# First mixer of a two-layer hybrid decoder: 12 of 16 input blocks multiplied whole, compression in column groups, two convolution steps moved between the steps of the attention

## Chip, cores and metric

One core of a Trainium2 chip runs the whole forward pass for 256 tokens of width 1024. The metric is the device time of one execution in microseconds; the time of a kernel is the median of its runs.

## What is computed

Two layers over a residual stream of 256 tokens. Layer 0's mixer, cut to what matters here:

```python
z = hn @ w_in                                   # hn = rmsnorm(x); 2328 columns
val, gate, q, kc, vc, ks, vs, kw, vw, g = split(z)
a = val * sigmoid(gate)                         # 512 channels
a_out = silu(layernorm(causal_conv31(a)))       # depthwise, 31 taps
k_cmp = gelu(blocks(kc) @ cmp_w1[0]) @ cmp_w2[0]   # 15 blocks of 32 tokens, 2 groups
v_cmp = gelu(blocks(vc) @ cmp_w1[1]) @ cmp_w2[1]
b_out = sigmoid(g) . (attn(q, k_cmp, v_cmp), attn(q, ks, vs), attn(q, kw, vw))
h = x + concat(a_out, b_out) @ w_out
```

Attention has 8 query heads and 2 key heads of 64; with 256 tokens the selected and the window branch both see all earlier tokens. Layer 1 mixes with trailing means instead. After each mixer comes a product-key mixture of 16384 experts (the bulk of the time: every expert's two rows, 512 KB for 128 experts, pass through TensorE), then a gated embedding. Everything is float32.

## The kernel before

Activations lie transposed (channels on partitions, 256 tokens along the row), and weights come in blocks of 128x1024 f32 (512 KB): eight 128x128 pieces that give one 128-column slice of the output. `plan` lists all blocks in order of use; `fetch` loads the next one through the SP queue into a ring of buffers (`RINGS`: 3 in the first mixer, 10 afterwards), and `refill` fetches as long as the ring has room.

There are two ways to multiply a block. **Split** (`u_block`, `mm3`): `prep_h` makes a rounded high half on ScalarE (L184), `prep_l` the low half on VectorE (L197), two blocks ahead, and then frees the ring's buffer; TensorE runs three reduced-precision products for each of the 8 pieces (L225 to L227), the activations being split into hnH and hnL at the start. **Whole** (`u_dense`, L248): eight f32 products straight from the ring's buffer, each of which the trace shows as two instructions; the buffer comes free when they are done. Before the change all 16 blocks of the first mixer's input projection (`win`), the 8 of its output projection (`wout`) and the 8 of the query projection (`wq`) are split; the expert tables are whole.

`mixer_even` first does four convolution groups, each with a value block and a gate block, evacuation, tanh, and the gated input `ap[c]` (L474 to L496). Then the loop over `STEPS` (L748) emits the rest: `C` the compressed keys and values (with shifts of E through POOL's queue), `K` the keys, `Q` the queries, `B` the blocks for the compression, `S` the split of the token weights `wt`, `W` values and gates by token, `M` the compression, `s`, `p`, `w` scores, compressed scores and weighing, `T` the part of the convolution taps that TensorE does (diagonal matrices made on ScalarE, L441; products L442; `PE_TAPS` of them per group), `L` one of three parts of the convolution's norm. The other taps are VectorE instructions (L459), one after another for each group; `taps(n)` emits the next n behind a step (`BEHIND_CONV` 6, `BEHIND_STEP` 3, `BEHIND_HALF` 5). The output projection (L760) takes the attention's four pieces first, then the convolution's.

A compression (`compress`, L565) contracts 32 tokens x 64 channels as 16 products of 30 columns (2 groups x 15 blocks) by 256, accumulated in 30 partitions of one bank; then gelu, two transposes, and the second weight.

The order on the SP and POOL queues is that of the program. On TensorE, VectorE and ScalarE a scheduler orders what is ready by the place in the program; an engine works off its queue in order.

Of the kernel before, what the change touches and what calls it, by code (L numbers as in the profile page):

```python
# [20 lines left out]
T = 256  # L21
# [14 lines left out]
RINGS, ROWBUFS, AHEAD = (3, 10), 7, 8  # L36
# [19 lines left out]
class Trunk:  # L56
# [72 lines left out]
    def plan(self):  # L129
# [22 lines left out]
        self.split_range(0, at["wq", 0] + 7)  # L152
# [90 lines left out]
    def u_dense(self, k, x):  # L243

        w = self.raw_block(k)
        out = self.bank()[:, :ND]
        for kt in range(KT):
            m = self.nc.tensor.matmul(out, w[:, kt * 128:kt * 128 + 128], x[:, kt, :ND],  # L248
                                      start=kt == 0, stop=kt == KT - 1)
        self.last_mm[k] = m  # L250
        self.raw_done(k)
        return out
# [145 lines left out]
    def mixer_even(self, st):  # L398
# [3 lines left out]
        base = self.at["in"]  # L402

# [70 lines left out]
        for c in range(4):  # L474
            pv = self.u_block(base + 2 * c)
# [4 lines left out]
            pg = self.u_block(base + 2 * c + 1)  # L480
# [19 lines left out]
        def in_kc(c):  # L500

            pk = self.u_block(next(nxt))
# [6 lines left out]
            blk.append((mp.tile([128, 16, 2, 15], F32, name=f"blk{c}"), E))  # L509
# [5 lines left out]
        def in_k(c):  # L515
            pk = self.u_block(next(nxt))
# [4 lines left out]
        def blocks(c):  # L521
            bt, E = blk[c]
            for g in range(2):
                v = E[g][:, 1:257].rearrange("p (n r) -> p r n", r=16)
                for hf in range(2):
                    pos = cpos[:, c, hf * 8:hf * 8 + 8, None].to_broadcast([128, 8, 15])
                    nc.vector.tensor_tensor(out=bt[:, hf * 8:hf * 8 + 8, g],
# [4 lines left out]
        def in_q(c):  # L532
            pq = self.u_block(next(nxt))
# [3 lines left out]
        wtH = mp.tile([128, KT, 280], F32R, name="wtH")  # L537
        wtL = mp.tile([128, KT, 280], F32R, name="wtL")
        vt = mp.tile([128, 2, 256], F32, name="vt")
        gt = mp.tile([128, 2, 24], F32, name="gt")  # L540

        def split_wt():
            for hf in range(2):
                s = slice(hf * 4, hf * 4 + 4)
                nc.scalar.activation(wtH[:, s], wt[:, s], AF.Copy)
                nc.vector.tensor_tensor(out=wtL[:, s], in0=wt[:, s], in1=wtH[:, s].bitcast(F32),
                                        op=ALU.subtract)
# [17 lines left out]
        def compress(c):  # L565

            ph = self.bank()
            for lp in range(16):
                nc.tensor.matmul(ph[0:30, :256], blk[c][0][:, lp].rearrange("p g n -> p (g n)"),  # L569
                                 w1[c][:, lp], start=lp == 0, stop=lp == 15)  # L570
            hid = mp.tile([30, 256], F32, name="hid", bufs=1)
            nc.scalar.activation(hid, ph[0:30, :256], AF.Gelu_apprx_tanh)
            pt = self.bank()
            for m in range(2):
                nc.tensor.transpose(pt[:, m * 32:m * 32 + 30], hid[:, m * 128:m * 128 + 128],
                                    self.ident[0:30, 0:30])
            hT = mp.tile([128, 2, 32], F32, name="hT", bufs=2)
            nc.scalar.activation(hT[:, :, 0:30],
                                 pt[:, 0:64].rearrange("p (m n) -> p m n", m=2)[:, :, 0:30], AF.Copy)
# [165 lines left out]
        steps = {"T": pe_taps, "C": in_kc, "K": in_k, "Q": in_q, "B": blocks, "S": split_wt,  # L745
                 "W": in_token, "M": compress, "p": compressed, "s": scores, "w": weigh}
        nxt = iter(range(base + 8, base + 16))
        for step in STEPS:  # L748
# [5 lines left out]
            if step[0] in "CKQWMpsw":  # L754
                taps(BEHIND_STEP)
# [697 lines left out]
```

## Time and profile before

| | us |
|---|---|
| median of 3 runs (lowest, highest) | 1530.15 (1526.87, 1534.93) |
| the profiled execution | 1531.44 |
| its span, first to last instruction | 1529.7 |
| mean granted TensorE clock | 0.993 |

The profile gives, for one execution, busy times of the engines, the waits and what ended them, and the chain of work that ended last. PE is TensorE, PEld its weight loads, DVE VectorE, ACT ScalarE, POOL GpSimd, SP SyncE. A matmul's recorded duration overlaps with the next one's, so the time that it costs is read from one start to the next. A few per cent of the records can be missing: of 108 VectorE taps the trace shows 106. The line in a row is that of the instruction, which may stand in a helper.

### The profile page before, as it was taken

Reading aid. Unit: us, or ns where it says so; the run is one execution under the profiler, and the core shown is the slowest. Engines: PE = TensorE matmul, PEld = TensorE weight load, DVE = VectorE, ACT = ScalarE, POOL = GpSimd, SP = SyncE. Lnnn points to the kernel's source line nnn. Section 1 sums busy time; section 2 is a strip of 40 time slices with the busy share of each in tenths; the row PEclk is TensorE's granted clock in tenths of the full one; section 3 lists DMA queues with packets and bytes.
Section 4 is the critical chain, followed back from the end, with each engine's and each line's share of the span. In section 5 each row is a group of like instructions: output and inputs, shape, how many; then the busy total and the mean of one; then the engine's idle time right before and its main releaser. Section 6 shows DMA issues by size and latency. Waiting matters only on the chain.

```text
span 1529.7 us, 30252 instructions
## 1 busy us (share of the span) xinstructions
PE 1499.5 (98%) x11882; PEld 1457.0 (95%) x11882; DVE 1142.0 (75%) x2752; ACT 684.7 (45%) x864; POOL 446.1 (29%) x406
## 2 busy tenths in 40 slices
PE   8999999999999999999998999999999999999997
PEld 8858999999999999999998999999999999999997
DVE  6997699988876888544448699987886788644446
ACT  6468321358863876000036321248872877000025
POOL 0000014343444333444300004343444333343400
PEclk9999999999999999999999999999999999999998
DMA  6603679999999999999985279999999999999980
GB/s 239 231 1 113 233 238 409 408 408 408 408 396 396 402 381 378 405 409 408 409 347 166 89 231 400 408 409 408 409 388 393 409 380 367 408 408 409 409 315 28
DMA packets 141245, 514.83 MB, mean 337 GB/s; under 512 B 15984, under 2 KB 16240, under 8 KB 140592
## 3 DMA queue, kind: packets, MB, share of 16 engines
q1 hardware_dynamic: 84384, 308.42, 52.6%
q0 software_dynamic: 55568, 202.66, 33.7%
q8 instruction: 94, 1.54, 0.4%
q10 hardware_dynamic: 1152, 1.82, 0.4%
q14 instruction: 47, 0.39, 0.1%
HBM read 511.53 MB, written 1.05 MB: 335 GB/s over the span
## 4 chain that ended last, share of the span: by engine, by line
PE 76%; DMA 12%; DVE 10%; ACT 1%; issue 1%; DVEq 0%; SPq 0%; ACTq 0%
PE bank_a L1015 28%; PE bank_a L248 26%; DMA wx<-in_v 9%; PE bank_g L1246 5%; PE bank_a L225 3%; PE bank_a L226 3%; PE bank_a L227 3%; DMA wx<-in_u 3%; DVE row L1341 2%; PE bank_a L569 1%; DVE rt_tmp L1033 1%; PE bank_a L640 1%; DVE yc L459 1%; PE bank_r L306 1%; DVE wL L197 1%
## 5 line engine op out<-in xcount | busy, mean ns | idle before, releaser
L1015 PE MATMUL bank_a<-z,wx 128*128 128x160 f32 x4096 | 574.6, 301 | 3.9 <-DMA wx<-in_v 1.0
L248 PE MATMUL bank_a<-hn,wx 128*128 128x160 f32 x4096 | 569.8, 300 | 2.1 <-DVE rt_gs L1204 1.2
L1015 PEld LDWEIGHTS bank_a<-z,wx 128*128 128x128 f32 x4096 | 559.3, 190 | 11.1 <-DMA wx<-in_v 11.0
L248 PEld LDWEIGHTS bank_a<-hn,wx 128*128 128x128 f32 x4096 | 558.7, 190 | 4.9 <-issue 1.8
L1235 ACT ACTIVATE o<-sq 128x512 fp8e4<-128x512 f16 x160 | 398.6, 2599 | 46.7 <-DVE sq L1227 46.5
L1314 POOL DMA_INDIRECT row<-in_ur,sp_idx x192 | 228.2, 1188 | 475.4 <-PE bank_a L248 193.7
L1351 DVE SCALAR_TENSOR_TENSOR sp_acc<-row,sp_w,sp_acc 128x1024 f32<-128x1024 f32 x188 | 241.7, 1286 | 153.1 <-DMA row<-in_v,sp_idx 152.4
L1314 POOL DMA_INDIRECT row<-in_v,sp_idx x192 | 210.0, 1094 | 333.8 <-PE bank_a L1015 220.3
L1341 DVE SCALAR_TENSOR_TENSOR row<-row,sp_x 128x1024 f32<-128x1024 f32 x192 | 231.1, 1217 | 31.5 <-DMA row<-in_ur,sp_idx 31.5
L184 ACT ACTIVATE wH<-wx 128x1024 fp32r<-128x1024 f32 (+1 forms) x63 | 65.4, 1042 | 389.0 <-DMA wx<-in_proj 338.1
L1008 ACT ACTIVATE z<-bank_a 128x160 f32<-128x160 f32 x256 | 95.8, 379 | 285.9 <-PE bank_a L248 285.2
L1251 DVE SCALAR_TENSOR_TENSOR z<-bank_g,z 128x512 f32<-128x512 f32 x80 | 93.1, 1163 | 66.2 <-PE bank_g L1246 66.2
L197 DVE TENSOR_TENSOR wL<-wx,wH 128x1024 fp32r<-128x1024 f32 (+1 forms) x63 | 75.8, 1204 | 50.9 <-ACT wH L184 50.4
L225 PE MATMUL bank_a<-hnH,wH 128*128 128x256 f32 x320 | 93.5, 295 | 6.0 <-ACT wH L184 5.6
L227 PE MATMUL bank_a<-hnH,wL 128*128 128x256 f32 x320 | 93.0, 292 | 0.3 <-DVE wL L197 0.3
L226 PE MATMUL bank_a<-hnL,wH 128*128 128x256 f32 x320 | 92.8, 291 | 0.0
L1246 PE MATMUL bank_g<-sq,o 128*128 128x64 f16 x1280 | 89.5, 237 | 0.0
L1246 PEld LDWEIGHTS <-o 128*128 128x128 fp8e4 x1280 | 82.6, 113 | 3.0
L1231 DVE TENSOR_TENSOR sq<-o,gHL 128x512 f16<-128x512 f16 x160 | 68.0, 425 | 11.1
L225 PEld LDWEIGHTS bank_a<-hnH,wH 128*128 128x128 f32 x320 | 63.2, 199 | 7.0 <-ACT wH L184 5.8
L1227 DVE TENSOR_TENSOR sq<-iota,i2T 128x512 f16<-128x512 f16 x160 | 67.2, 420 | 0.0
L227 PEld LDWEIGHTS bank_a<-hnH,wL 128*128 128x128 f32 x320 | 63.6, 199 | 0.7 <-DVE wL L197 0.6
(313 smaller groups left out, 1208.6 us busy)
## 6 DMA issues: line engine op xcount, KB each, us to landing
wx<-in_u SPq DMA_DIRECT2D x256, 512.0 KB, 13.1
wx<-in_v SPq DMA_DIRECT2D x256, 512.0 KB, 11.6
wx<-in_wq SPq DMA_DIRECT2D x16, 512.0 KB, 3.7
wx<-in_gatew SPq DMA_DIRECT2D x16, 512.0 KB, 6.5
wx<-in_win SPq DMA_DIRECT2D x15, 512.0 KB, 6.1
w<-in_cw SPq DMA_DIRECT2D x2, 2048.0 KB, 9.9
wx<-in_wout SPq DMA_DIRECT2D x8, 512.0 KB, 3.8
row<-in_ur,sp_idx POOLq DMA_INDIRECT x192, 9.6
```

What stands on the lines that cost most here:

```text
L225: mm(out, wH, xH, start=start, stop=False, **kw)
L226: mm(out, wH, xL, start=False, stop=False, **kw)
L227: mm(out, wL, xH, start=False, stop=stop, **kw)
L248: m = self.nc.tensor.matmul(out, w[:, kt * 128:kt * 128 + 128], x[:, kt, :ND], start=kt == 0, stop=kt == KT - 1)
L1008: self.nc.scalar.activation(z[i // HB][:, i % HB], ps, AF.Gelu_apprx_tanh)
L1015: m = self.nc.tensor.matmul(acc[kt // 2][:, (kt % 2) * ND:(kt % 2) * ND + ND], w[:, kt * 128:kt * 128 + 128], x, start=b == 0 and kt % 2 == 0,
L1235: nc.scalar.activation(o8.rearrange("p t e -> p e t"), o2, AF.Copy, saturate=False)
L1246: nc.tensor.matmul(ps[k][:, c:c + HB], o8[:, t], og[:, p, :, t], start=p == 0, stop=p == 1)
L1251: nc.vector.scalar_tensor_tensor(v, ps.pop(k).rearrange("p (t b) -> p t b", b=HB), 1.0 / GSCALE, v, op0=ALU.mult, op1=ALU.mult)
L1314: ins = k.nc.gpsimd.indirect_dma_start(out=G, out_offset=None, in_=table, in_offset=bass.IndirectOffsetOnAxis(ap=self.idx[:, c:c + 1], axi ...
L1341: nc.vector.scalar_tensor_tensor(G, G, 1.0, self.x[u], op0=ALU.mult, op1=ALU.mult, accum_out=self.dot[:, col])
L1351: nc.vector.scalar_tensor_tensor(self.acc[u], G, self.w[:, col], self.acc[u], op0=ALU.mult, op1=ALU.add)
```

## The change

Four blocks stay split (`SPLIT = 4`, the first two convolution groups). The other twelve go through `u_whole`, which reads a new copy `hx` of the scaled activations (eight ScalarE copies). The token groups use `wt` whole, so step `S` is gone. The ring has four buffers instead of three. The convolution groups become steps `V0` to `V3` in `STEPS`; `V2` now stands behind `K1` and `V3` behind `M1`; the loads of `w1` move from the convolution groups to `C0` and `C1`. The splits of the output projection start after `V3`. `PE_TAPS` changes from 6 and 8 to 4 and 12. In the compression the 16 products are spread over four groups of 32 partitions; a product with `self.sel[1]`, a 128x32 matrix of four stacked identities, sums the groups and transposes in one step, and gelu follows it.

```diff
-RINGS, ROWBUFS, AHEAD = (3, 10), 7, 8
+RINGS, ROWBUFS, AHEAD = (4, 10), 7, 8
+SPLIT = 4
...
-STEPS = ("T1 Q1 C0 C1 K0 K1 B1 Q0 Q2 T3 B0 S W1 Q3 s0 M0 s1 W0 s2 p0 M1 w0 L w1 s3 p1 w2 L w3 L"
-         .split())
-PE_TAPS = (0, 6, 0, 8)
+STEPS = ("V0 V1 T1 C0 C1 K0 K1 V2 Q0 Q1 B1 B0 s0 W0 M0 s2 Q2 Q3 W1 s1 M1 V3 T3 p0 p1 s3 w0 w1 L w2 L"
+         " w3 L".split())
+PE_TAPS = (0, 4, 0, 12)
...
-        self.split_range(0, at["wq", 0] + 7)
+        self.split_range(0, SPLIT - 1)
...
-    def u_dense(self, k, x):
+    def u_whole(self, k, x, n):
...
+        hx = mp.tile([128, KT, T], F32, name="hx")
...
-        for c in range(4):
-            pv = self.u_block(base + 2 * c)
+        def block(k):
+            return self.u_block(k) if k < SPLIT else self.u_whole(k, hx, T)
+
+        def in_conv(c):
+            pv = block(next(nxt))
...
+            pg = block(next(nxt))
             if c == 0:
                 self.stats_close(st, then=AF.Tanh)
+                for kt in range(KT):
+                    nc.scalar.activation(hx[:, kt], self.h[:, kt], AF.Copy,
+                                         scale=self.vecs[:, V_MIX[0], kt:kt + 1])
...
             if c == 1:
                 nc.sync.dma_start(wt, a["wtok"])
-            elif c > 1:
-                nc.sync.dma_start(w1[c - 2], a["cw1"][c - 2])
-            taps(BEHIND_CONV)
...
         def in_kc(c):
-            pk = self.u_block(next(nxt))
+            pk = self.u_whole(next(nxt), hx, T)
...
-            blk.append((mp.tile([128, 16, 2, 15], F32, name=f"blk{c}"), E))
+            bt = mp.tile([128, 16, 32], F32, name=f"blk{c}")
+            nc.gpsimd.memset(bt[:, :, 30:32], 0.0)
+            blk.append((bt, E))
+            nc.sync.dma_start(w1[c], a["cw1"][c])
...
             for kt in range(KT):
-                self.mm3(pv, self.hnH[:, kt, s], self.hnL[:, kt, s], wtH[:, kt], wtL[:, kt],
-                         kt == 0, kt == KT - 1)
+                nc.tensor.matmul(pv, hx[:, kt, s], wt[:, kt], start=kt == 0, stop=kt == KT - 1)
...
-            ph = self.bank()
+            ph = self.bank()[:, :256]
             for lp in range(16):
-                nc.tensor.matmul(ph[0:30, :256], blk[c][0][:, lp].rearrange("p g n -> p (g n)"),
-                                 w1[c][:, lp], start=lp == 0, stop=lp == 15)
-            hid = mp.tile([30, 256], F32, name="hid", bufs=1)
-            nc.scalar.activation(hid, ph[0:30, :256], AF.Gelu_apprx_tanh)
-            pt = self.bank()
+                q = lp % 4 * 32
+                nc.tensor.matmul(ph[q:q + 32], blk[c][0][:, lp], w1[c][:, lp], start=lp < 4,
+                                 stop=lp >= 12, skip_group_check=True)
+            hid = mp.tile([128, 256], F32, name="hid", bufs=1)
+            nc.scalar.activation(hid, ph, AF.Copy)
+            pt = self.bank()[:, :64]
             for m in range(2):
-                nc.tensor.transpose(pt[:, m * 32:m * 32 + 30], hid[:, m * 128:m * 128 + 128],
-                                    self.ident[0:30, 0:30])
+                nc.tensor.matmul(pt[:, m * 32:m * 32 + 32], hid[:, m * 128:m * 128 + 128],
+                                 self.sel[1], start=True, stop=True)
...
+            nc.scalar.activation(hT.rearrange("p m n -> p (m n)"), pt, AF.Gelu_apprx_tanh)
...
-        nxt = iter(range(base + 8, base + 16))
+        nxt = iter(range(base, base + 16))
...
+            if step == "V3":
+                self.split_range(self.at["wout"], self.at["wq", 0] + 7)
+                self.prep_l(self.at["wout"] + 1)
+            if step[0] in "VCKQWMpsw":
+                taps(BEHIND_CONV if step[0] == "V" else BEHIND_STEP)
```

The steps `K` and `Q` call `u_whole` in the same way, and the blocks of `win` are stored in the order in which `STEPS` names them.

## Rows read from the trace of the kernel before

**Rows 1.** The page, its first part: busy us, share of span, instructions of each engine

```profile
PE 1499.5 (98%) x11882; PEld 1457.0 (95%) x11882; DVE 1142.0 (75%) x2752; ACT 684.7 (45%) x864; POOL 446.1 (29%) x406
```

**Rows 2.** Windows by stage, whole kernel; columns: stretch, length, busy us per engine, clock, DMA

```profile
0.00:28.00 28.00, 22.44 (x134) 21.96 (x135) 15.21 (x44) 17.03 (x33) 3.46 (x13) 0.88 0.59 197
28.00:73.00 45.00, 44.37 (x336) 42.13 (x335) 44.26 (x89) 20.79 (x33) 2.31 (x4) 1.00 0.72 265
73.00:128.80 55.80, 54.25 (x323) 32.62 (x322) 50.02 (x155) 42.52 (x123) 0.00 (x0) 1.00 0.06 20
128.80:152.00 23.20, 23.18 (x192) 23.17 (x193) 19.31 (x38) 16.50 (x33) 0.80 (x2) 1.00 0.52 160
```

**Rows 3.** Groups by line, 28 to 128.8 us: busy, mean ns, idle before

```profile
L459 DVE SCALAR_TENSOR_TENSOR yc<-ap,cvec,yc 128x256 f32<-128x256 f32 x106 | 47.1, 475 | 0.2
L227 PE MATMUL bank_a<-hnH,wL 128*128 128x256 f32 x97 | 27.7, 286 | 0.3 <-DVE wL L197 0.3
L197 DVE TENSOR_TENSOR wL<-wx,wH 128x1024 fp32r<-128x1024 f32 x13 | 15.8, 1217 | 0.3 <-ACT wH L184 0.3
L184 ACT ACTIVATE wH<-wx 128x1024 fp32r<-128x1024 f32 x13 | 13.7, 1056 | 14.8 <-PE bank_a L226 5.3 <-DMA wx<-in_wout 3.4 <-DMA wx<-in_win 3.1
```

**Rows 4.** Chain that ended last, mixer: start us, us to the next piece, what

```profile
30.18 0.12 PE bank_a L225
39.54 0.86 PE bank_g L442 x4
72.09 0.13 PE bank_a L225
...
75.97 7.04 PE bank_a L569 x32
90.90 0.86 PE bank_a L640 x2
118.53 1.75 PE bank_a L684 x16
```

**Rows 5.** Timeline of PE, column groups and tiles: start us, us, line, operands

```profile
107.03 1.08 PE L692 MATMUL bank_g<-PT,vt 128*64 128x256 f32 x8
108.05 0.61 PE L674 MATMUL bank_a<-ident,Pc 128*15 128x128 f32 x4
...
180.39 0.67 PE L1063 MATMUL bank_g<-sub,qT 64*32 64x128 f32 x32
180.99 1.22 PE L248 MATMUL bank_a<-hn,wx 128*128 128x160 f32 x7
```

**Rows 6.** Timelines of DVE and PE, fourth convolution group: evacuation, gating, then its taps

```profile
41.00 0.42 DVE L472 TENSOR_TENSOR th<-bank_a,rs 128x256 f32<-128x256 f32 x1
43.26 0.42 DVE L488 SCALAR_TENSOR_TENSOR ap<-th,val 128x256 f32<-128x256 f32 x1
...
64.10 1.03 PE L442 MATMUL bank_g<-ap,dg 128*128 128x256 f32 x4
67.06 1.13 PE L442 MATMUL bank_g<-ap,dg 128*128 128x256 f32 x4
```

**Rows 7.** Timelines of DVE and PE: last tap, row broadcast, projection start

```profile
107.50 0.48 DVE L459 SCALAR_TENSOR_TENSOR yc<-ap,cvec,yc 128x256 f32<-128x256 f32 x1
125.37 1.41 DVE L734 TENSOR_TENSOR yc<-yc,bank_r 128x256 f32<-128x256 f32 x4 [1.79 <-PE bank_r L338]
...
128.82 0.62 PE L225 MATMUL bank_a<-hnH,wH 128*128 128x256 f32 x3 [0.49 <-ACT hnH L699]
```

**Rows 8.** Waits, 28 to 128.8 us: who for whom, total us, times, longest

```profile
ACT wH L184 <- DMA wx<-in_win: 3.1, 1, 3.1
ACT hT L578 <- PE bank_a L575: 1.6, 2, 1.2
```

**Rows 9.** DMA issues: count, KB each, median us to landing

```profile
wx<-in_win SPq DMA_DIRECT2D x15, 512.0 KB, 6.1
w<-in_cw SPq DMA_DIRECT2D x2, 2048.0 KB, 9.9
```

More of the change, by code (lines that the diff above doesn't have):

```diff
@@ L241, in u_block @@
         return out
-    def u_dense(self, k, x):
+    def u_whole(self, k, x, n):
         w = self.raw_block(k)
-        out = self.bank()[:, :ND]
+        out = self.bank()[:, :n]
         for kt in range(KT):
-            m = self.nc.tensor.matmul(out, w[:, kt * 128:kt * 128 + 128], x[:, kt, :ND],
+            m = self.nc.tensor.matmul(out, w[:, kt * 128:kt * 128 + 128], x[:, kt, :n],
                                       start=kt == 0, stop=kt == KT - 1)
@@ L515, in in_k @@
         def in_k(c):
-            pk = self.u_block(next(nxt))
+            pk = self.u_whole(next(nxt), hx, T)
             for g in range(2):
@@ L526, in blocks @@
                     pos = cpos[:, c, hf * 8:hf * 8 + 8, None].to_broadcast([128, 8, 15])
-                    nc.vector.tensor_tensor(out=bt[:, hf * 8:hf * 8 + 8, g],
+                    nc.vector.tensor_tensor(out=bt[:, hf * 8:hf * 8 + 8, g * 15:g * 15 + 15],
                                             in0=v[:, 0::2, hf:hf + 15], in1=pos, op=ALU.add)
@@ L532, in in_q @@
         def in_q(c):
-            pq = self.u_block(next(nxt))
+            pq = self.u_whole(next(nxt), hx, T)
             nc.vector.scalar_tensor_tensor(qT[c], pq, 0.125, self.rs, op0=ALU.mult, op1=ALU.mult)
-        wtH = mp.tile([128, KT, 280], F32R, name="wtH")
-        wtL = mp.tile([128, KT, 280], F32R, name="wtL")
         vt = mp.tile([128, 2, 256], F32, name="vt")
         gt = mp.tile([128, 2, 24], F32, name="gt")
[L542 to L547, printed above, removed]
         def in_token(tt):
@@ L744, in mixer_even @@
         ln = conv_norm()
-        steps = {"T": pe_taps, "C": in_kc, "K": in_k, "Q": in_q, "B": blocks, "S": split_wt,
+        steps = {"V": in_conv, "T": pe_taps, "C": in_kc, "K": in_k, "Q": in_q, "B": blocks,
                  "W": in_token, "M": compress, "p": compressed, "s": scores, "w": weigh}
-        nxt = iter(range(base + 8, base + 16))
+        nxt = iter(range(base, base + 16))
         for step in STEPS:
@@ L753, in mixer_even @@
                 steps[step[0]](*map(int, step[1:]))
-            if step[0] in "CKQWMpsw":
-                taps(BEHIND_STEP)
+            if step == "V3":
[3 more added lines that the diff above has]
+                taps(BEHIND_CONV if step[0] == "V" else BEHIND_STEP)
         st = self.stats_open()
@@ L898, in peer_and_ple @@
             step(self.GATE_NS if i > HB else self.DENSE_NS if sparse.ready else self.ROUTE_NS)
-            ps = self.u_dense(base + i, hn)
+            ps = self.u_whole(base + i, hn, ND)
             if pend is not None:
@@ L1394, in layout @@
     qh = q.reshape(D, 2, 4, 64)
-    cols = []
-    for c in range(4):
-        cols += [val[:, 128 * c:128 * c + 128], gate[:, 128 * c:128 * c + 128]]
-    named = {"C0": kc, "C1": vc, "K0": ks, "K1": kw}
-    named.update({f"Q{j}": qh[:, :, j].reshape(D, 128) for j in range(4)})
-    cols += [named[n] for n in STEPS if n in named]
+    named = {"C0": (kc,), "C1": (vc,), "K0": (ks,), "K1": (kw,)}
+    named.update({f"Q{j}": (qh[:, :, j].reshape(D, 128),) for j in range(4)})
+    named.update({f"V{c}": (val[:, 128 * c:128 * c + 128], gate[:, 128 * c:128 * c + 128])
+                  for c in range(4)})
+    cols = [x for n in STEPS if n in named for x in named[n]]
     a["win"] = f(np.stack([_cols(c) for c in cols]))
```

3 lines of the change are left out of this document (removed).

## The prediction

> **What bounds the kernel now.** I read the page first [rows 1]: TensorE is busy for 98% of the span. Busy time of pipelined matmuls overstates the work, so the stage has to be read by start-to-start times. The windows by stage [rows 2] are next: the change touches only the first mixer, that is the stretch up to 128.8 us (where the output projection begins), and, through the buffers, the 23.2 us of projection behind it. From 28 us, where the four blocks that stay split have passed, to 128.8 us the reader sees VectorE busy for 94.3 of 100.8 us (44.3 + 50.0), ScalarE for 63.3, and the DMA engines busy for 72% and then 6%. So two engines could be the bound, TensorE and VectorE.
>
> The groups of that stretch [rows 3] say what fills VectorE: 106 recorded convolution taps, 47.1 us; 13 subtractions for the low half of a weight block, 15.8 us. ScalarE spends 13.7 us on the 13 high halves.
>
> For TensorE I add up start-to-start times from the chain and the timeline [rows 4, 5]: a split matmul 0.12 us, so a split block (24) 2.88 us; a 280-column one 0.13 us, so a token group (24) 3.15 us; a convolution tap in whole f32 (two instructions of 256 columns) 0.43 us; a compression 7.04 us; a score product 0.86 us and its mask 0.11; a 128-column transpose 0.11 us; a two-column-group instruction 0.128 us. The stretch from 28 us then holds 12 blocks (34.6), 14 taps (6.0), 2 token groups (6.3), 2 compressions (14.1, and about 1.0 of short products), 12 score products with masks (11.6), 16 products for the compressed scores (1.7, taken at the transpose's 0.11), the weighing with 64 transposes and 64 paired instructions (7.0 + 8.2) and the convolution norm with 8 long and 20 short ones (1.7 + 2.2): 94.4 us of 100.8. **TensorE is the bound**, dense to 94%; about 6.4 us are waits. VectorE is nearly as full but seldom in its way. Everything behind the mixer starts from its last product, and nothing of it is edited, so I carry a microsecond there as a microsecond of the span.
>
> **The change part by part.** *Twelve whole blocks.* Each loses 24 products at 0.12 us (2.88) and gains 8 f32 products of 256 columns. The chain has that shape: the tap, 0.86 us for four instructions with the next following at once, and the compression, 32 in 7.04 [rows 4]. So 16 x 0.216 = 3.46 us, 0.58 more per block, **+6.9 us on TensorE** for twelve. It takes 12 x 1.22 = 14.6 us from VectorE and 12 x 1.06 = 12.7 us from ScalarE [rows 3], two of the twelve ahead of 28 us, and adds eight scaled copies on ScalarE (hx). I cost those at nothing: a copy of 128x1024 takes 1.06 us [rows 3], so eight quarters of it are some 2 to 4 us, ScalarE is idle for 11 of the first 28 us [rows 2], and hx is first read at about 28 us. Without that cover it is those 2 to 4 us, once.
>
> *Token groups whole.* 24 products at 0.13 become 8 f32 products of 280 columns, 16 x 0.216 x 280/256 = 3.78 us instead of 3.15: **+1.3 us** for both. The splitting of wt (four instructions) goes too; none of it is on the path.
>
> *Taps.* PE_TAPS goes from 14 to 16: **+0.9 us** on TensorE, two taps less on VectorE (about 0.9 us).
>
> *Compression in column groups.* Now 32 instructions of 30 output columns, one behind another, in 7.04 us. After the change four neighbours write four groups of 32 partitions. The trace has no such four; it has neighbours. Two groups of 64 (the weighing): 8 instructions in 1.02 us, 0.128 us instead of 0.22 [rows 5], a factor of 1.7 out of 2. Tiles of 64x32: 32 instructions of 128 columns in 0.60 us [rows 5], 0.019 against 0.109 for a whole one [rows 4], 5.8 out of 8. At 0.72 to 0.85 of a factor of 4 a compression takes 2.1 to 2.4 us. Bounds: 1.76 (a full four) and 4.1 (no better than two groups). I take 2.2, the nearest rows being those with several tiles at work: **-9.6 us** for both, between -10.6 and -5.9. The Trainium skill (TensorEngine Tiling (Array Packing), Theoretical Speedup) gives up to 4x for 32 columns; by that the term would be -10.6 us.
>
> The same rows speak against a full gain: eight paired instructions at 0.216 a pair would be 0.86 us, and 1.02 pass before the next form starts [rows 5], some 0.15 us at a change of form. Four such changes are 0.6 us, inside the value taken. The Trainium skill (same page, Key Properties) states that changing the tiling mode drains the engine; the row agrees in kind, and no row here isolates its price.
>
> The sum of the groups moves from a transpose to a product with sel[1], four short instructions instead of two; gelu moves behind it, the copy of 128x256 before it replaces a gelu of the same width. I take these as zero, with 0.3 us either way per compression.
>
> TensorE's work: +6.9 + 1.3 + 0.9 - 9.6 = **-0.5 us**, between -1.5 and +3.2.
>
> *Waits.* Of the 6.4 us, some go: the subtraction of wtL, a tap mixed between split products, and the weight preparation behind ScalarE. Others stay: the two hand-overs to ScalarE inside a compression (1.6 us of idle ScalarE before hT [rows 8] shows their size). I take **-1 us**, between -4 (only the compression's own hand-overs and the switches stay) and 0.
>
> *Order and queues.* Steps V2 and V3 (two blocks each, then tanh and gating) move behind K1 and M1. Each carries its evacuations (L472 to L488), the SP queue's refills, and V3 carries the start of the output projection's splits (two high, two low halves, 2.1 us of ScalarE, 2.4 us of VectorE), now in the last third instead of in the middle. VectorE has some 16 us less to do in this stage, so it hides them. On SP the two loads of w1 (2 MB each) move ahead, behind the fetches that blocks C0 and C1 release; fetches behind them wait. A load of w1 lands in 9.9 us, a block in 6.1 [rows 9]. The ring holds four blocks, so a block's fetch is issued some three blocks (10.4 us) ahead, and by my count the tightest one (the second block of V2) has 4 us left. Zero, with 1 us as the far bound; before the change one such delay was 3.1 us of ScalarE's time and reached nobody [rows 8]. POOL gets two small memsets behind the shifts of E; its queue then only waits for the routing.
>
> **Sum.** -0.5 - 1 = -1.5 us. The profiled execution took 1531.44 us, its span is 1529.7 us, the rest lies around it and is not edited; the median of the three runs is 1530.15, 1.3 us below. On the median: 1530.15 - 1.5, so about **1528.5 us**.
>
> **The rivals.**
>
> *A. The tail becomes the bound (slower).* The convolution of channel group 3 starts only when V3 is done. Adding the steps from 28 us in the new order (T1 1.7, six blocks 20.7, Q0 Q1 6.9, s0 1.9, W0 3.8, M0 3.2, s2 3.9, Q2 Q3 6.9, W1 3.8, s1 1.9, M1 3.2, V3 6.9) V3 ends at 93 us. From the product's evacuation to the gated input takes 2.7 us [rows 6]: 95.7. T3 now has 12 taps; eight took 3.8 us [rows 6], so 12 take 5.7, or up to 7 where other products stand between: 101 to 103. Nineteen VectorE taps follow at 0.40 alone or 0.59 when another instruction stands between: last tap at 109 to 114, against 108.0 now [rows 7]. Between the last tap and the projection lie 20.8 us now (108.0 to 128.8 [rows 7]); kept whole, the projection would get its last inputs 1 to 6 us later than now. For it: 0.5 us of TensorE's wait at 128.82 is already put down to ScalarE's hnH, and VectorE waits 1.8 us for the row broadcast just before [rows 7], so this chain is late now. Against: in those 20.8 us each step waits for weighing steps put ahead of it, counted by their own instructions alone they add to about 14 (an estimate); and the attention halves of the first three projection blocks (3 x 12 x 0.12 = 4.3 us) can run before the convolution's. It decides from a last tap later than about 112 us. Price +2 to +6, at the middle **1534 us**.
>
> *B. The relief counts (faster).* VectorE loses some 16 of 94 us (ten of the twelve subtractions at 1.22, the two of wt at about 1.3, two taps). If the waits fall to their lower bound and the four groups run in full, -1.5 - 4 = -5.5 us: **1524.5 us**. Against: VectorE's fullness shows in few of TensorE's waits now.
>
> *C. The column groups do less than said.* With pairs only the compression gives -5.9 instead of -9.6: work +3.2, waits -1, **1532.5 us**. With none beside another it gives nothing: +9.1 - 1, **1538 us**. The 64x32 rows [rows 5] speak against both.
>
> *D. A transfer is late* behind w1: +3 to +5 us, **1533 us**, against it the 4 us of reserve.
>
> **How the numbers follow.** Forecast (between -4 and +1 us) 0.48, A 0.22, B 0.14, C 0.10 (0.03 of it with no groups at all), D 0.03, something that I don't see 0.03. A measurement can tell 0.5% (7.65 us) from no change, that is under 1522.5 and over 1537.8. Before's own three runs lie 8 us apart, so a true -5.5 is read as faster now and then, and a true +6 as slower: half of B and a little of the forecast make faster 0.11; the worse half of A, the no-groups case of C and a part of what I don't see make slower 0.13; same 0.76. For 8 in 10 the range reaches from B with some spread, 1521, to the far end of A with it, 1537.
>
> **What would show it.** Right: a whole block at 16 instructions in about 3.46 us where now 24 take 2.88; a compression's 32 products in 1.8 to 2.4 us; VectorE's share between 28 and 110 us down from full to about 80%; the projection starting between 125 and 129 us; nothing changed in the stages behind but the offset. A: TensorE idle before the projection, waiting for hnH of the convolution channels, with the last tap behind 112 us. B: a projection that starts before 124 us. C: 32 compression products in 4 or 7 us. D: a wait of TensorE for a transfer of win or of w1. I am wrong in kind if a stage behind the mixer changes its length, or if the clock granted in the mixer does (1.00 from 28 us on [rows 2]).

## The result, and the profile after

The changed kernel takes 1546.99 us (median of 6 runs, 1545.54 to 1551.39), the kernel before in the same series 1530.8 us (6 runs, 1526.87 to 1534.93). The ratio is 1.0116, with a 95% interval of 1.0097 to 1.0136: slower by some 17 us, outside the range that I gave. The profiled execution took 1548.81 us, its span is 1547.0 us, 17.3 more than before.

The windows by stage, core 0 of the changed kernel (stretch, length, busy us of PE, PEld, DVE, ACT and POOL, granted clock, share of the DMA engines, GB/s). The bounds are the first score (63.4), the end of the first attention steps, the end of V3's products (111.5) and the output projection (140.0 to 171.0). Below the dots stand two short stretches at the lower clock:

```profile
29.00:63.40 34.40, 29.71 (x138) 25.55 (x137) 30.17 (x76) 3.46 (x8) 2.57 (x6) 1.00 0.68 252
63.40:84.80 21.40, 17.93 (x86) 9.87 (x86) 17.99 (x47) 10.60 (x37) 0.00 (x0) 0.76 0.00 1
84.80:111.50 26.70, 25.67 (x146) 19.96 (x146) 14.69 (x50) 10.98 (x35) 0.00 (x0) 1.00 0.36 119
111.50:140.00 28.50, 28.50 (x179) 17.93 (x178) 16.60 (x44) 20.95 (x56) 0.00 (x0) 1.00 0.06 19
140.00:171.00 31.00, 27.91 (x202) 27.01 (x202) 22.43 (x50) 20.65 (x40) 0.80 (x2) 0.89 0.35 120
...
64.50:71.40 6.90, 4.83 (x9) 2.67 (x9) 6.02 (x15) 2.84 (x16) 0.00 (x0) 0.51 0.00 0
78.20:81.60 3.40, 3.40 (x13) 1.63 (x13) 2.50 (x8) 1.64 (x4) 0.00 (x0) 0.50 0.02 5
```

Against [rows 2] three things are new. TensorE is idle for 9.2 of the 111.0 us from 29 to 140 (111.0 less 29.71, 17.93, 25.67 and 28.50), before for 2.2 of 100.8. Its granted clock falls to half twice in this stretch, where it was full before. And the projection, 23.2 us long at full clock before, takes 31.0 at 0.89, although nothing in it is edited.

That gives the account. The projection starts at 140.0 instead of 128.8, 11.2 us later: 1.0 from the first whole block (28.95 instead of 28), 7.0 from idle TensorE, 4.1 from the half clock (half of the 4.83 and of the 3.40 us that it worked at it), which leaves -0.9 for the work itself. The projection adds 7.8. From there to the expert tables it is 29.0 us in both. Of the 19.0 us, 17.3 reach the end.

TensorE's timeline (start us, duration us, engine, line, operands, count, and in brackets the idle time before and what ended it):

```profile
28.95 2.32 PE L251 MATMUL bank_a<-hx,wx 128*128 128x256 f32 x10
...
33.27 18.29 PE L251 MATMUL bank_a<-hx,wx 128*128 128x256 f32 x84
52.87 7.14 PE L251 MATMUL bank_a<-hx,wx 128*128 128x256 f32 x32 [1.31 <-DMA wx<-in_win]
63.39 1.10 PE L642 MATMUL bank_a<-kz,qT 128*128 128x512 f32 x2 [3.37 <-DVE qT L544]
...
66.80 2.07 PE L642 MATMUL bank_a<-kz,qT 128*128 128x512 f32 x2 [2.07 <-DVE qT L544]
...
74.09 1.93 PE L571 MATMUL bank_a<-w,blk 128*32 128x256 f32 x32
76.53 0.63 PE L578 MATMUL bank_a<-sel,hid 128*128 128x32 f32 x4 [0.50 <-ACT hid L574]
78.06 0.55 PE L586 MATMUL bank_a<-hT,w 128*64 128x15 f32 x8 [0.90 <-ACT hT L581]
...
104.52 7.17 PE L251 MATMUL bank_a<-hx,wx 128*128 128x256 f32 x32
...
113.36 1.03 PE L446 MATMUL bank_g<-ap,dg 128*128 128x256 f32 x4
...
121.99 0.60 PE L446 MATMUL bank_g<-ap,dg 128*128 128x256 f32 x2
...
146.44 0.63 PE L228 MATMUL bank_a<-hnH,wH 128*128 128x256 f32 x3 [0.90 <-ACT hnH L742]
...
152.93 0.39 PE L228 MATMUL bank_a<-hnH,wH 128*128 128x256 f32 x1 [1.44 <-ACT wH L187]
...
154.19 0.58 PE L230 MATMUL bank_a<-hnH,wL 128*128 128x256 f32 x1 [0.75 <-DVE wL L200]
```

What was costed is as costed: 84 instructions of whole blocks at 0.216 us from one start to the next (18.29 us less the last one's recorded 0.38, by 83), and 32 products of a compression in 1.93 us instead of the 7.04 of [rows 4]. The first scores are what is late: the last query block ends at 59.8, and the two score products with their masks, 1.9 us of work, last until 69.1, with two waits for qT. VectorE's timeline shows why:

```profile
42.05 0.36 DVE L537 TENSOR_TENSOR blk<-E,cpos 128x120 f32<-128x120 f32 x1 [1.54 <-DMA E<-E]
...
45.34 0.36 DVE L537 TENSOR_TENSOR blk<-E,cpos 128x120 f32<-128x120 f32 x1 [1.88 <-DMA E<-E]
...
53.82 0.42 DVE L476 TENSOR_TENSOR val<-bank_a,rs 128x256 f32<-128x256 f32 x1
...
59.14 3.77 DVE L463 SCALAR_TENSOR_TENSOR yc<-ap,cvec,yc 128x256 f32<-128x256 f32 x9
62.82 0.42 DVE L544 SCALAR_TENSOR_TENSOR qT<-bank_a,rs 128x256 f32<-128x256 f32 x1
63.16 3.26 DVE L463 SCALAR_TENSOR_TENSOR yc<-ap,cvec,yc 128x256 f32<-128x256 f32 x8
66.32 0.43 DVE L544 SCALAR_TENSOR_TENSOR qT<-bank_a,rs 128x256 f32<-128x256 f32 x1
...
111.73 0.42 DVE L476 TENSOR_TENSOR th<-bank_a,rs 128x256 f32<-128x256 f32 x1 [3.03 <-PE bank_a L251]
...
122.62 0.48 DVE L460 SCALAR_TENSOR_TENSOR yc<-ap,cvec,bank_g 128x256 f32<-128x256 f32 x1 [0.87 <-PE bank_g L446]
...
133.02 1.52 DVE L463 SCALAR_TENSOR_TENSOR yc<-ap,cvec,yc 128x256 f32<-128x256 f32 x3
```

It stood 3.4 us for the shifts of E, with everything behind it in its queue: the value block of V2 was evacuated at 53.82, though its product had ended at 48. The taps that fill the time of a product each came late too, nine ahead of the first qT and eight ahead of the second. In the last third the fourth group's rows of [rows 6, 7] are found again, much later: its gate block is evacuated at 111.73 instead of 41.00, its twelve taps on TensorE run from 113.36 to 122.5, where eight had begun at 64.10, and VectorE's 19 taps run from 122.6 to 134.5, where the last one was over at 108.0 before. From there to the first product with the convolution's half at 146.44 it is another 11.9 us.

The projection itself then holds 3.1 us of idle TensorE (31.00 less 27.91). Of these, 0.90 are the wait for the convolution's half. The other two waits, 1.44 and 0.75, are for halves of a weight block: ScalarE makes them behind a square of the projection's first result, for which it had stood 1.51 us:

```profile
151.51 0.42 ACT L285 ACTIVATE sq<-h 128x256 f32<-128x256 f32 x1 [1.51 <-DVE h L767]
```

From about 153 to 160 us the clock is at half.

The DMA issues from 28 to 62 us (count, KB each, median us to landing) belong to VectorE's wait and to TensorE's of 1.31 us; the last line is from the same view of the kernel before, in a fence of its own, and blocks of `win` landed in 7.4 us there:

```profile
wx<-in_win SPq DMA_DIRECT2D x8, 512.0 KB, 9.0
w<-in_cw SPq DMA_DIRECT2D x2, 2048.0 KB
E<-E POOLq DMA_DIRECT2D x4, 64.0 KB, 6.4
```

```profile
E<-E POOLq DMA_DIRECT2D x4, 64.0 KB, 4.3
```

### The profile page after: what moved, and what is told of

Same layout as the page of the kernel before. It is cut to its first block, busy times and chain, and to the rows that moved or that the text cites. A ratio compares the mean times of both kernels' runs of the same rounds, so it can differ in the third digit from the quotient of the medians.

```text
span 1547.0 us, 29993 instructions
## 1 busy us (share of the span) xinstructions
PE 1506.3 (97%) x11778; PEld 1459.3 (94%) x11778; DVE 1129.2 (73%) x2736; ACT 673.0 (44%) x858; POOL 450.7 (29%) x408
## 4 chain that ended last, share of the span: by engine, by line
PE 68%; DVE 16%; DMA 12%; ACT 2%; issue 1%; POOL 0%; SPq 0%; DVEq 0%; ACTq 0%
PE bank_a L1020 28%; PE bank_a L251 22%; DMA wx<-in_v 9%; PE bank_g L1251 5%; DVE row L1346 4%; PE bank_a L228 3%; PE bank_a L230 3%; PE bank_a L229 3%; DVE yc L463 2%; DVE rt_tmp L1038 1%; DMA wx<-in_u 1%; DVE rt_ixd L1042 1%; PE bank_a L642 1%; DMA row<-in_ur,sp_idx 1%; PE bank_g L694 1%
## 5 line engine op out<-in xcount | busy, mean ns | idle before, releaser
L1240 ACT ACTIVATE o<-sq 128x512 fp8e4<-128x512 f16 x160 | 398.7, 2600 | 47.0 <-DVE sq L1232 45.8
L187 ACT ACTIVATE wH<-wx 128x1024 fp32r<-128x1024 f32 (+1 forms) x51 | 52.9, 1038 | 383.1 <-DMA wx<-in_proj 337.7
L200 DVE TENSOR_TENSOR wL<-wx,wH 128x1024 fp32r<-128x1024 f32 (+1 forms) x51 | 61.1, 1203 | 51.5 <-ACT wH L187 50.4
L228 PE MATMUL bank_a<-hnH,wH 128*128 128x256 f32 x224 | 66.4, 304 | 8.0 <-ACT wH L187 7.1
L230 PE MATMUL bank_a<-hnH,wL 128*128 128x256 f32 x224 | 66.7, 301 | 1.5 <-DVE wL L200 1.5
L229 PE MATMUL bank_a<-hnL,wH 128*128 128x256 f32 x224 | 66.5, 300 | 0.0
L228 PEld LDWEIGHTS bank_a<-hnH,wH 128*128 128x128 f32 x224 | 45.6, 207 | 8.8 <-ACT wH L187 7.3
## 6 DMA issues: line engine op xcount, KB each, us to landing
wx<-in_v SPq DMA_DIRECT2D x256, 512.0 KB, 10.6
```

What stands on the lines that cost most here:

```text
L228: mm(out, wH, xH, start=start, stop=False, **kw)
L229: mm(out, wH, xL, start=False, stop=False, **kw)
L230: mm(out, wL, xH, start=False, stop=stop, **kw)
L1240: nc.scalar.activation(o8.rearrange("p t e -> p e t"), o2, AF.Copy, saturate=False)
```

## The experiments

The theory behind the first ones: the **order** made the loss. V3 behind M1 makes the convolution's tail late (rival A, larger than I priced it), and the loads of w1, moved ahead, delay what is fetched beside them (rival D). The rivals: the whole blocks cost more than their work, or the column groups give less than their work. Each time stands with its ratio to the kernel before in the same series. The kernel before lay at 1530.8 us beside the changed kernel, at 1527.56 beside w1_late, v3_early, old_order and cmp_alone, at 1530.06 beside both_moved, old_compress, cmp_filled and covered, and at 1530.37 beside the rest, so gains and losses below are differences of ratios, taken of 1530 us. The last two columns and all rows are of one profiled execution, whose own time stands under "profiled" and is up to 6.4 us off the median.

| | us | ratio (95% interval) | profiled | last tap | projection, length |
|---|---|---|---|---|---|
| before | 1530.8 | | 1531.44 | 108.0 | 128.8, 23.2 |
| changed | 1546.99 | 1.0116 (1.0097 to 1.0136) | 1548.81 | 134.5 | 140.0, 31.0 |
| w1_late | 1540.23 | 1.0086 (1.0069 to 1.0102) | 1541.39 | 127.8 | 133.3, 29.7 |
| v3_early | 1531.42 | 1.0027 (1.0011 to 1.0042) | 1531.82 | 90.5 | 129.8, 23.2 |
| both_moved | 1537.5 | 1.0050 (1.0033 to 1.0066) | 1536.43 | 89.4 | 138.6, 23.2 |
| all_split | 1533.15 | 1.0025 (1.0013 to 1.0037) | 1537.8 | 121.5 | 127.5, 30.9 |
| old_compress | 1559.26 | 1.0194 (1.0177 to 1.0211) | 1552.82 | 142.8 | 148.4, 28.4 |
| old_order | 1531.85 | 1.0029 (1.0016 to 1.0042) | 1533.93 | 91.0 | 131.5, 23.2 |
| whole_alone | 1538.09 | 1.0055 (1.0038 to 1.0072) | 1535.98 | 89.3 | 136.6, 23.2 |
| cmp_alone | 1538.34 | 1.0072 (1.0052 to 1.0091) | 1543.67 | 119.4 | 139.2, 27.0 |
| cmp_filled | 1534.34 | 1.0032 (1.0018 to 1.0046) | 1532.0 | 111.2 | 129.6, 25.5 |
| covered | 1543.01 | 1.0091 (1.0072 to 1.0110) | 1540.18 | 88.4 | 137.2, 25.5 |
| lean_old | 1529.4 | 0.9996 (0.9984 to 1.0007) | 1531.18 | 95.4 | 129.1, 23.2 |
| lean_new | 1528.63 | 0.9985 (0.9976 to 0.9995) | 1528.97 | 96.9 | 126.9, 23.2 |

### v3_early

```diff
-... K0 K1 V2 Q0 Q1 ... s1 M1 V3 T3 p0 ...
+... K0 K1 V2 V3 T3 Q0 Q1 ... s1 M1 p0 ...
```

> The changed kernel with V3 and T3 moved up, right behind V2; all else as it is. Theory 2 (late V3): the output projection took 31.0 us instead of 23.2 because the convolution's last taps end 26 us later than before; with V3 early the last tap ends before 115 us, the output projection takes 23 to 25 us, and the time falls by 6 to 9 us, to 1538 to 1541. Theory 1 (transfers at the start) alone: nothing moves at the first scores, the time stays within 3 us of 1547.

Measured: 1.0027, some 13.6 us less than the changed kernel (0.89% of 1530), from two steps of `STEPS` alone. Its windows (columns as above):

```profile
29.00:72.20 43.20, 39.74 (x183) 34.29 (x182) 42.07 (x103) 8.92 (x20) 2.58 (x6) 1.00 0.60 213
72.20:100.70 28.50, 26.98 (x141) 17.99 (x139) 20.05 (x51) 14.53 (x49) 0.00 (x0) 1.00 0.34 112
100.70:129.80 29.10, 28.42 (x222) 18.44 (x221) 17.78 (x70) 25.61 (x73) 0.00 (x0) 1.00 0.00 1
129.80:153.00 23.20, 23.20 (x193) 23.20 (x194) 19.32 (x38) 16.43 (x33) 0.80 (x2) 1.00 0.48 160
```

The projection is back at 23.2 us and the clock full throughout. Last tap and projection are as the theory of the late V3 expected, but the gain is larger than its 6 to 9 us. It is more than the tail: TensorE no longer waits for qT, nor VectorE for the shifts of E. VectorE's adds on E begin at 45.8 there instead of 42.05, and two more blocks pass on TensorE ahead of the queries, in which VectorE can catch up; that this is why is argued, not shown. TensorE's waits fall to 5.7 us (100.8 less 39.74, 26.98 and 28.42), of which 1.71 for a block of win and 1.75 for V3's gating.

### w1_late

```diff
-            nc.sync.dma_start(w1[c], a["cw1"][c])         # in in_kc: C0, C1
+            if step in {'Q0': 0, 'Q1': 1}:
+                nc.sync.dma_start(w1[n], a["cw1"][n])
```

> The changed kernel with one edit: the two loads of w1 (2 MB each) are issued behind Q0 and Q1 instead of behind C0 and C1. Theory 1 (transfers): in the changed kernel the loads of w1 slow the shifts of E and the fetch of Q0's block; VectorE stands 3.4 us for E in its queue and falls about 6 us behind, so Q0's and Q1's evacuations come late and TensorE idles about 7 us at the first scores, where its clock also falls. Then the wait of VectorE for E is gone, the first scores start near 60 us instead of 63.4, and the time falls by 6 to 11 us, to 1536 to 1541. Theory 2 (late third convolution group alone): the loss is in the tail, the time stays within 3 us of 1547. Theory 3 (the planned order of VectorE's queue alone, taps ahead of the evacuations): the first scores still start 3 us or more behind the end of Q1's product, and the time falls by less than 4 us.

Measured: 1.0086, about 4.6 us less than the changed kernel: between what theories 1 and 3 gave. The first score starts at 58.98 instead of 63.39, as theory 1 said. The wait for a block of win, VectorE's for E and the first of the two for qT are gone. The second stays, as TensorE's timeline shows:

```profile
62.29 1.12 PE L641 MATMUL bank_a<-kz,qT 128*128 128x512 f32 x2 [2.07 <-DVE qT L543]
```

So the loads of w1 did hold up the shifts and a block of win. The tail stays late behind the scores: last tap 127.8, a projection of 29.7 us.

### both_moved

Both edits together.

> The changed kernel with both moves undone: V3 and T3 directly behind V2, and the two loads of w1 issued behind Q0 and Q1. If the order alone made the loss (late V3, early w1) and my sum for TensorE holds (-0.5 of work, -1 of waits): the 1.7 us wait for a block of win that was left with V3 early is gone as well, the projection starts at 127 to 129 us and the time is 1527 to 1530 us. If the sum is wrong, because TensorE's waits did not get less: the projection starts at 130 or later, 1531 to 1534 us.

Measured: 1.0050, slower than V3 early alone; both expectations failed, since w1 is now late. The row of TensorE's timeline with the first compression, then the windows around the stretch at half clock:

```profile
82.93 3.64 PE L569 MATMUL bank_a<-w,blk 128*32 128x256 f32 x32 [4.70 <-DMA w<-in_cw]
```

```profile
29.00:80.80 51.80, 47.11 (x212) 39.36 (x210) 50.70 (x124) 14.78 (x43) 2.57 (x6) 1.00 0.44 154
80.80:94.50 13.70, 10.60 (x52) 5.09 (x53) 9.68 (x24) 5.82 (x13) 0.00 (x0) 0.50 0.58 243
94.50:138.60 44.10, 43.42 (x288) 29.71 (x286) 21.22 (x78) 29.12 (x88) 0.00 (x0) 1.00 0.07 25
```

The first load of w1 was issued only at 72.8, behind three refills of the output projection in SP's queue. The wait is 4.7 us, and in the middle of it the clock goes to half for 13.7 us, which costs half of the 10.6 us worked there. The place of these two loads has two wrong sides, ahead of the blocks and behind the refills.

### all_split

```diff
-            return self.u_block(k) if k < SPLIT else self.u_whole(k, hx, T)
+            return self.u_block(k)                         # C, K and Q in the same way
```

> The changed kernel with all 16 input blocks split as before, the new order and the column groups kept. By my sum TensorE has 6.9 us less to do: 1539 to 1541 us. If in this order VectorE's queue is what TensorE waits for (twelve subtractions of 1.22 us more on it, ahead of the same taps): 1548 us or more, the last tap later than 134, the first score later than 63.

The output projection's splits, too, simply follow those of the input blocks here, instead of starting behind V3.

Measured: 1.0025, below both expectations: in the new order the whole blocks cost 13.9 us, not 6.9, although they relieve VectorE. The first score comes at 55.1 instead of 63.4, no wait for a block of win is left, and only 0.3 us of waiting for qT; VectorE's adds on E stand at 57.68 and later instead of from 42.05, behind its subtractions, and wait for nothing. Rows of TensorE, VectorE and the projection's window:

```profile
55.12 1.02 PE L642 MATMUL bank_a<-kz,qT 128*128 128x512 f32 x2
...
57.68 0.35 DVE L537 TENSOR_TENSOR blk<-E,cpos 128x120 f32<-128x120 f32 x1
...
127.50:158.40 30.90, 27.94 (x202) 26.95 (x202) 22.30 (x50) 20.65 (x40) 0.80 (x2) 0.89 0.35 120
```

So a VectorE with more to do is not what TensorE waits for; these rows speak for what stands in its queue ahead of a late transfer, though the edit also changes when buffers come free. The tail stays late all the same: with 12.5 us less in front of it the projection still takes 30.9 us in the profiled execution, which was the longest of the ten, 4.7 us over the median.

### old_compress

The compression of before, in the changed kernel.

> The changed kernel with the compression of before (32 products of 30 columns one behind another) in the new order. V3 still stands behind M1, so all that a compression takes longer delays V3, its convolution and the projection: by the order theory +9.6 us of the two compressions, 1555 to 1558 us, last tap 141 to 146. If the clock behind the column groups costs as much as they save: 1545 to 1550 us, with no half clock between 70 and 85 us.

Measured: 1.0194, 12 us above the changed kernel and somewhat above both ranges, last tap 142.8. By the ratios the column groups give there about what they save (10.2 us, twice 7.04 less 1.93), and the clock doesn't take it back. The profiled execution, the shortest of the four, shows less: its projection starts 8.4 us later than in the changed kernel, and its own time is 4.0 us longer.

### old_order and whole_alone

```diff
-STEPS = ("V0 V1 T1 C0 C1 K0 K1 V2 Q0 ...   PE_TAPS = (0, 4, 0, 12)
+STEPS = "V0 V1 V2 V3 T1 Q1 C0 C1 K0 K1 B1 Q0 Q2 T3 B0 W1 Q3 s0 M0 s1 W0 ..."   PE_TAPS = (0, 6, 0, 8)
```

Both have the order of before, with w1 loaded behind V2 and V3 and the splits of wout behind Q3; whole_alone has the old compression besides.

> The changed kernel (twelve whole blocks, tokens whole, compression in column groups, ring of four) in the old order: all four convolution groups first, the old steps, 6 and 8 taps on TensorE, the loads of w1 behind V2 and V3, the output projection's splits begun behind the last block. If the order is what costs (theories 1 and 2 together), TensorE's sum holds again: 1524 to 1531. If whole blocks themselves cost it (twelve at 3.46 us and a buffer that stays taken until the products are done), it stays at 1540 or above.

> The order and the compression of before, the taps on TensorE of before (14), with twelve whole blocks and whole token groups: what the whole blocks do alone. By my sum +6.9 and +1.3 of work on TensorE, less some waits: 1536 to 1539 us. If VectorE was in TensorE's way in the kernel before (the relief of 16 us counts): 1531 to 1534 us, with the last tap at 90 to 95 instead of 108. Beside the same order with the compression in column groups as well (1531.9 us) it also says what the column groups give there: 9.6 us by my sum, which would be 1541 us here, or next to nothing if the clock takes it back.

Measured: whole_alone 1.0055 (1.0038 to 1.0072), 8.4 us, against +8.2 by my sum (6.9 and 1.3). VectorE's last tap came 18.7 us earlier and that gave nothing: rival B falls. old_order 1.0029, just above the range that the order theory gave: the old order, with its taps and its place of the loads of w1, takes away 13 of the changed kernel's 18 us. The column groups give 4.0 us here, not 9.6, with a clock of 0.91 from 83 to 103 us behind the waits of the first compression.

### cmp_alone and cmp_filled

cmp_alone is the kernel before with the new compression and nothing else. cmp_filled adds products that nobody reads:

```diff
             nc.scalar.activation(hid, ph, AF.Copy)
+            fill = self.bank()[:, :256]
+            for q in range(4):                             # three more behind the product with sel
+                nc.tensor.matmul(fill, self.ident, w1[c][:, q], start=True, stop=True)
```

> The kernel before with one part of the change: the compression in four column groups. If TensorE bounds the mixer before the change, a compression's 32 products take 1.8 to 2.4 us instead of 7.0 and the time falls by 6 to 10 us, to 1521 to 1525. If VectorE bounds it (it is full from 35 to 110 us), TensorE only waits more and the time falls by less than 3 us.

> The kernel before with the compression in column groups alone, and with TensorE kept at work in the compression's two hand-overs to ScalarE: four full products of 128x256 f32 (0.43 us each) behind the 32 products, three more behind the product with sel, into a bank that nobody reads. 3 us of work more in each compression, 6 us together, of which the hand-overs (2.5 us of idle TensorE in each) hide most. If the clock is what made the compression alone slow (granted half for four stretches of 3 to 10 us behind such gaps): the clock stays at full from 23 us to the projection, which starts at 127 to 132 us instead of 139, and the time is 1528 to 1533 us although TensorE has more to do. If VectorE is what made it slow: 1538 to 1543 us, the projection at 139 or later. If both: the clock full and the projection between 133 and 138.

Measured: the compression alone makes the kernel slower, 1.0072, which neither expectation had. With 6 us of useless work added it is at 1.0032: the intervals do not meet. The two kernels are 6 us apart by the ratios; the rows below exaggerate that, because the profiled execution of cmp_alone was the longest of its four and that of cmp_filled a short one of its ten (1543.67 and 1532.0). Windows of cmp_alone, then of cmp_filled:

```profile
73.00:105.00 32.00, 26.95 (x171) 16.46 (x170) 29.34 (x86) 22.62 (x71) 0.00 (x0) 0.81 0.05 16
105.00:139.20 34.20, 30.75 (x150) 17.38 (x149) 17.39 (x63) 18.50 (x46) 0.00 (x0) 0.78 0.05 16
```

```profile
73.00:105.00 32.00, 31.76 (x225) 21.30 (x224) 31.67 (x95) 22.86 (x72) 0.00 (x0) 1.00 0.02 6
105.00:129.60 24.60, 21.41 (x121) 13.84 (x121) 13.90 (x50) 16.92 (x43) 0.00 (x0) 0.86 0.07 23
```

And TensorE's waits around the first and the second compression in cmp_alone:

```profile
78.52 0.63 PE L580 MATMUL bank_a<-sel,hid 128*128 128x32 f32 x4 [1.58 <-ACT hid L576]
80.05 0.62 PE L588 MATMUL bank_a<-hT,w 128*64 128x15 f32 x8 [0.90 <-ACT hT L583]
...
100.70 1.03 PE L678 MATMUL bank_a<-ident,Pc 128*15 128x128 f32 x4 [2.57 <-DVE Pc L626]
```

At the end of its second compression cmp_alone was 7 us ahead of the kernel before (97.5 against 104.5); the rest up to the projection took 41.7 us instead of 24.3. In the old order VectorE is full (29.34 of 32.0), and the faster TensorE waits: 1.58 and 0.90 us for ScalarE inside the first compression, 2.57 for VectorE behind the second. The clock falls to half behind these waits (0.50 from 100 to 106 us), and much of the weighing runs at half. The filling keeps the clock full up to 105 us. About 5 us stay over the kernel before, with 3.2 us of waits for the convolution's norm behind VectorE's last tap (111.2) and a fall of the clock behind them; that this part is VectorE's is argued from these rows. So neither expectation held whole: the projection starts at 129.6, as for the clock alone, but the clock isn't full up to it.

### covered, lean_old and lean_new

```diff
+... K1 V2 V3 Q0 T3 Q1 B1 B0 s0 M0 W0 X0 s2 Y0 Q2 Q3 M1 W1 X1 s1 Y1 p0 ...   # covered: compress cut into M, X, Y; w1 behind Q0, Q1
+PE_TAPS = (0, 4, 0, 4)                                                       # lean_old: old_order
+... K1 V2 V3 Q0 T3 Q1 B1 B0 s0 W0 M0 ...   PE_TAPS = (0, 4, 0, 4)           # lean_new: w1 behind V2, V3
```

> As both moves undone, and besides: T3 one block later (behind Q0, so that TensorE does not wait for V3's gating, 1.8 us), and the compression cut into three steps with other steps between them (M0 W0 X0 s2 Y0 and M1 W1 X1 s1 Y1), so that other products stand in its hand-overs to ScalarE (1.6 to 2.4 us of idle TensorE in each). If the waits of TensorE are what is left: another 3 to 5 us less than with both moves undone, 1523 to 1527 us, the projection at 123 to 126 us. If the end is set by the weighing's own chain (scores, ScalarE, transposes) or by the convolution norm: no less than with both moves undone, 1527 to 1531 us.

Measured: 1.0091. The first compression, now ahead of W0, waited 6.1 us for w1, and the stretch from the second compression to the projection took 35.7 us with TensorE dense; both expectations failed, and whether covered hand-overs help was not settled.

> The order of before with whole blocks and column groups, and 8 instead of 14 taps on TensorE (PE_TAPS 0, 4, 0, 4): VectorE's last tap was at 91 there, some 20 us before it is needed, so TensorE gives it six taps back. If TensorE bounds that order: 6 x 0.43 = 2.6 us less, and up to 1.8 us of its wait for the fourth group's gating, 1527 to 1530 us, last tap at 93 to 97. If VectorE's queue still bounds the stretch up to the scores: no gain, 1531 to 1534 us.

> The changed kernel with V3 directly behind V2, T3 behind Q0, eight taps less on TensorE (PE_TAPS 0, 4, 0, 4) and the loads of w1 behind V2 and V3, between the place that made a block late (behind C0 and C1) and the one that made the compression late (behind Q0 and Q1). If the three waits found (1.7 us for a block of win, 1.8 us for the gating, 4.7 us for w1 with the half clock behind it) are what is left over my sum: full clock from 23 us on, the projection at 123 to 127 us, 1524 to 1528 us. If w1 is late at this place too: TensorE idle before the first compression, half clock behind it, 1532 to 1538 us.

Measured: lean_old 0.9996, no difference from before and 5 us less than old_order, as expected if TensorE bounds that order; its clock still fell around the first compression (0.83 from 80 to 100 us). lean_new 0.9985 (0.9976 to 0.9995), 2 us faster than the kernel before and about 20 faster than the changed one, the projection at 126.9 as expected and the time 0.6 us over its range:

```profile
29.00:69.40 40.40, 39.09 (x183) 33.82 (x183) 39.56 (x100) 4.97 (x12) 2.57 (x6) 1.00 0.62 226
69.40:98.00 28.60, 27.07 (x145) 18.07 (x147) 27.79 (x68) 15.73 (x50) 0.00 (x0) 1.00 0.34 114
98.00:126.90 28.90, 28.24 (x220) 18.29 (x220) 17.57 (x69) 25.43 (x73) 0.00 (x0) 1.00 0.01 1
126.90:150.10 23.20, 23.18 (x192) 23.18 (x193) 19.32 (x38) 16.49 (x33) 0.80 (x2) 1.00 0.50 160
```

TensorE waits for 3.5 of 97.9 us, the clock stays full, and the taps that TensorE no longer does end on VectorE at 96.9, well before they are needed.

## Why the prediction was wrong, by its own steps

**The work was right.** Whole blocks 3.46 us each, as said; token groups 3.77 (said 3.78); a compression 1.93, between the bounds of 1.76 and 4.1 and nearer to the full four than the 2.2 that I took; the work of TensorE together -0.9 us by the account above (said -0.5), and whole_alone at +8.4 for a term of +8.2. VectorE's share from 29 to 111.5 us fell to 76% (said 80% up to 110). The Trainium skill (TensorEngine Tiling (Array Packing), Theoretical Speedup) gives up to 4x for 32 columns; the trace shows 7.04 against 1.93 us, 3.6x.

**"Order and queues" failed.** I costed it at zero because VectorE has 16 us less to do. Two steps of it broke. First, the loads of w1: I looked at the blocks of win behind them (4 us left for the second block of V2, 1 us as the far bound; the trace shows a wait of 1.31, for Q0's block), and passed over POOL's queue, of which I noted two memsets. What was held up there was the shifts of E, and VectorE waited for them, with the evacuations of K0, K1, V2 and the queries queued behind it. That is rival D, by a way that I had not seen: w1_late, which moves only these two loads, gains 4.6 us. The shifts were in the kernel before and cost nothing there, so I never asked what would stand behind that wait in the new order. Second, V3: the ring's buffers and the splits were counted, the tail was left to rival A. v3_early, which moves only V3 and T3, gains 13.6 us.

**"Waits", -1 us, had the wrong sign.** I called 6.4 us of the stretch waits, the part that my sum of products did not fill; by the windows of [rows 2] TensorE was idle for only 2.2 of them, so there was little to gain. Its idle time grew by 7.0 us to 9.2: 5.4 for qT, 1.3 for win, and 2.4 for the compressions' own hand-overs (0.50, 0.90 and 1.03, where they were 0.46, 0.31 and 0.31 before).

**Rival A was the right mechanism, priced far too low (+2 to +6).** I let V3 end at 93 us; it ended at 111.5. Of the 18.5 us, some 18.2 are found: 1.0 is the later start, 9.2 TensorE's waits, 4.1 the half clock, and 3.9 are products of the compressed scores and of the convolution's mean, which stand ahead of it and which I had left out. Its twelve taps took 9.1 us instead of 5.7 to 7, the 19 on VectorE 0.63 us each (said up to 0.59), the last one at 134.5 instead of 109 to 114. The point from which it decides was about right: with the last tap at 108 us or before, the projection takes 23.2 us (covered apart, whose weighing is in another order), at 111.2 it takes 25.5, and from 119 on 27 to 31. Its price came out as a projection of 31.0 us instead of 23.2, not as a late start of it: 0.90 us for the convolution's halves, which come at 146.4, 2.2 for the weight halves behind them, up to 3.4 of half clock, and the rest mostly short products that now stand between (202 instructions instead of 192). That all_split and w1_late, with earlier tails, keep 30 us speaks for V3's place as the cause, not the delays ahead of it, and v3_early's 23.2 us confirms it.

**The clock was not in the sum.** I carried 1.00 from 28 us on and named a fall as a sign of being wrong in kind. It cost 4.1 us ahead of the projection and up to 3.4 in it (6.8 us at half, from about 153 to 160).

**What held:** a microsecond at the end of the mixer is one at the end of the span, but for 1.7 of 19.0. Rivals B and C fell: B by whole_alone, C by the compression's 1.93 us. And with V3 early, w1 between its two wrong sides and eight taps less, the sum nearly comes out: -0.5 and another -3.4 (8 x 0.43) of work, +1.3 of waits, and +1.5 because the first whole block starts at 29.54 instead of 28, -1.1 us in all, where lean_new's projection starts 1.9 us earlier.

**Open:** how the loss divides between the E shifts and the queue of taps behind them. v3_early and all_split each take away both and nearly the same amount (13.6 and 13.9), so the shares do not add up; why the scheduler puts the adds on E so much later in all_split was not tried.

## What to carry to other kernels

A sum of work on the busiest engine says what a change can give; what it does give is set by the order in the queues, so walk each moved step through every queue and ask which late transfer now stands in front of which evacuation. A step whose result still has a long serial chain on another engine (a block, gating, 31 taps, a norm) cannot be moved behind the work that used to hide that chain. And before speeding up an engine in a stage where a second one is full, look at where the saved time turns into gaps: in these runs they were paid for once as waits and again as clock.

## What the hardware showed that I had not expected

The clock fell behind short waits. In cmp_alone it went to half at 79.1 us, right behind a wait of 1.58 us, and stayed there until 85.9. In the changed kernel it fell at 78.2, right behind the compression's waits of 0.50 and 0.90 us and 7 us after it had come back from the fall at the late scores; in lean_new the same two waits, behind a stretch with few gaps, left it full. And useless products in the gaps, 6 us of them, made a kernel 6 us faster (1.0072 to 1.0032), with the clock at 1.00 instead of 0.81 in the window around both compressions.

Shifts of 64 KB between partitions landed in 6.4 us instead of 4.3 beside two loads of 2 MB, although they go through another queue; blocks of 512 KB took 9.0 us, against 7.4 in the same stretch of the kernel before and 6.1 over all of it [rows 9].
